# Output projection of a hybrid decoder layer: three of four units as Strassen block products, the last unit tile by tile

## The chip, the cores and the metric

The kernel runs on one core of one Trainium2 chip. The metric is the device time of one launch in microseconds (us). Engines are named as in the profile: PE (TensorE matmul), PEld (its weight loads), DVE (VectorE), ACT (ScalarE), POOL (GpSimd) and SP (SyncE). SP issues most DMAs. DMAs that add into their destination ("accumulating") are issued on POOL's queue. Sixteen DMA engines serve all queues.

## The reference

One decoder layer for 1024 tokens of width 2048. A combined projection feeds a sparse attention (heads of group A) and a chunkwise mLSTM (group B). The two results, 1024 columns each, are joined and projected, and a residual and a layer norm follow:

```python
y = jnp.concatenate([y_a, y_m], axis=-1) @ w_out[l]
x = layer_norm(ALPHA * x + y, ln_g[l], ln_b[l])
```

The change touches the product with `w_out` (2048 x 2048), how its left operand is stored, and the norm's place.

## The kernel before

All large matmuls run at about fp32 accuracy by three passes: an operand `a` is split into a rounded high part and the low rest (`split`, lines 104 to 106: a copy on ACT, a subtraction on DVE), and `mm3` (lines 108 to 111) adds high x high, high x low and low x high into one PSUM bank. One matmul here has a 128x128 stationary tile and 512 moving columns.

The stages are: the first projection groups; then 19 projection units of four column groups each and the value projection (class `Values`, lines 727 to 822), both already as Strassen block products: seven products of 512x512 blocks in place of eight, with sums of weight blocks made on DVE, POOL or by accumulating DMA (lines 631, 736); then mLSTM, then attention (lines 1097 to 1241), then the output projection (lines 1244 to 1333). `y_d` in HBM holds the transposed left operand, 16 tiles of 128 x 1024: 0 to 7 from attention, 8 to 15 from mLSTM.

The output projection runs over two halves of 512 tokens (`half`) and four blocks of 512 output columns (`cb`). One such block is 16 contraction tiles (`kt`, mLSTM's first) x 4 token tiles (`t`) x 3 passes = 192 matmuls into four banks; eight blocks make 1536. Each block loads and splits its 16 weight tiles (`load_wo`). `load_y` loads and splits the left operand, half by half. `residual` adds ALPHA x and collects statistics (`bn_stats`). `norm` finishes one token tile: six 128x512 steps on DVE, and for the column block 3 two on ACT and two on POOL, then four stores. The first half's four norms run while PE computes the second half. The last block goes token tile by token tile, so that each tile's norm runs beside the next tile's matmuls.

The order of instructions is made by a planner. It takes priorities (`tc.high_priority`) and orders (`tc.issue_after`), and it hands out the buffers of a tag as they come free: `wraw` has 6 (loaded weights), `wh` and `wl` 4 each (split weights), `s4` 11 tiles of 4 KB a partition. The pool `oq` lies where attention's pool `ap` was. Matmuls of the output projection come after attention's last logits (`last_logit`) and fill PE between attention's last blocks.

Of the kernel before, what the change touches and what calls it, by code (L numbers as in the profile page):

```python
# [19 lines left out]
P = 128  # L20
# [79 lines left out]
def kernel(ctx, tc, a, out):  # L100
# [47 lines left out]
    part_d = dp.tile([NU, P, 2, T], F32, name="part_d")  # L148
    if_d = dp.tile([2 * H_M, T], F32, name="if_d")
# [744 lines left out]

    def mlstm_store(h, j, hs, sg):
        for half in range(2):
            ps = bank("ht")
            for c in range(4):
                pe.transpose(ps[:, c * P:(c + 1) * P], hs[half][:, c, j * P:(j + 1) * P], ident)
            vec.tensor_tensor(sg[:, halves[half]], ps, sg[:, halves[half]], op=OP.mult)  # L900
        sync.dma_start(y_d[8 + 2 * h + j], sg)
# [182 lines left out]
    HT = T // 2  # L1084
    yh, yl = {}, {}

    def load_y(q, half, pool_):
        with tc.high_priority(offset=O_PRIO):
            i = half, q
            yh[i] = pool_.tile([P, 2, HT], F32R, name=f"yh{q}")  # L1090
            yl[i] = pool_.tile([P, 2, HT], F32R, name=f"yl{q}")
            for k in range(2):
                raw = wp.tile([P, HT], F32, name="wraw", tag="wraw", bufs=WR)
                sync.dma_start(raw, y_d[2 * q + k, :, half * HT:(half + 1) * HT])
                split(yh[i][:, k], yl[i][:, k], raw)

    with ExitStack() as ph:
        ap = ph.enter_context(tc.tile_pool(name="ap", bufs=2))

        def head_inputs(h):  # L1100
            tb = ap.tile([P, 640], F32, name="tb")
# [3 lines left out]
            gt = ap.tile([P, T], F32, name="gt")  # L1105
# [3 lines left out]

        diagonal = [[ap.tile([P, 512], F32R, name=f"{n}{i}", bufs=1) for n in ("dh", "dl")] for i in range(2)]  # L1110
# [3 lines left out]
        head_0 = head_inputs(0)  # L1114
        mask = []
        for t in range(8):
            w = max((t + 1) * P, 256)
            m = ap.tile([P, w], BF16, name=f"mask{t}", bufs=1)
# [6 lines left out]
            mask.append(m)  # L1125
# [15 lines left out]
        def weights(p, qk, tb):  # L1141
# [3 lines left out]
            for t in (2 * p, 2 * p + 1):  # L1145
# [6 lines left out]
                pool.tensor_tensor(nm[:, 0:ws], mask[t][:, w - ws:w], tb[:, off:off + ws], op=OP.add)  # L1152
# [36 lines left out]
        def mix(b):  # L1189
# [11 lines left out]
            if b.kk == b.p:  # L1201
                s = slice(b.p * 256, (b.p + 1) * 256)
                vec.tensor_tensor(b.gt[:, s], out_ps[0], b.gt[:, s], op=OP.mult)
                if b.end:
                    sync.dma_start(y_d[b.h], b.gt)
# [34 lines left out]
        for q in range(4, 8):  # L1240
            load_y(q, 0, op)
# [3 lines left out]
    ln = []  # L1245
    for half in range(2):
        z = []
        for t in range(4):
            r0 = half * HT + t * P
            z.append([s4("z") for _ in range(2)])  # L1250
            for i in range(2):
                (pool if half else sync).dma_start(z[t][i], a["x"][r0:r0 + P, i * T:(i + 1) * T])

        def product(ps, t, kt, wh, wl, n):
            ts = slice(t * P, (t + 1) * P)
            return mm3(ps, yh[half, kt // 2][:, kt % 2, ts], yl[half, kt // 2][:, kt % 2, ts], wh, wl,
                       n == 0, n == KT - 1)

        def residual(t, cb, ps):
            zc = z[t][cb // 2][:, (cb % 2) * 512:(cb % 2) * 512 + 512]  # L1260
            vec.scalar_tensor_tensor(out=zc, in0=zc, scalar=ALPHA, in1=ps, op0=OP.mult, op1=OP.add)
            vec.bn_stats(st[t][:, cb], zc)

        def norm(t):
            mv = oq.tile([P, 2], F32, name="mv", bufs=2)
            vec.bn_aggr(mv, st[t])
            rs = oq.tile([P, 1], F32, name="rs", bufs=2)
            tt = oq.tile([P, 1], F32, name="tt", bufs=2)
            nmean = oq.tile([P, 1], F32, name="nmean")
            act.activation(tt, mv[:, 1:2], AF.Sqrt, bias=eps)  # L1270
            refine_rsqrt(rs, mv[:, 1:2], tt)
            r0 = half * HT + t * P
            for cb in (3, 0, 1, 2):
                zc = z[t][cb // 2][:, (cb % 2) * 512:(cb % 2) * 512 + 512]
                cs = slice((cb % 2) * 512, (cb % 2) * 512 + 512)
                g, b = ln[cb // 2][:, cs], ln[2 + cb // 2][:, cs]
                if cb == 3:
                    act.mul(nmean, mv[:, 0:1], -1.0)
                    act.activation(zc, zc, AF.Identity, bias=nmean)
                    pool.tensor_tensor(zc, zc, g, op=OP.mult)  # L1280
                    act.mul(zc, zc, rs)
                    pool.tensor_tensor(zc, zc, b, op=OP.add)
                else:
                    vec.scalar_tensor_tensor(out=zc, in0=zc, scalar=mv[:, 0:1], in1=g, op0=OP.subtract, op1=OP.mult)
                    vec.scalar_tensor_tensor(out=zc, in0=zc, scalar=rs, in1=b, op0=OP.mult, op1=OP.add)
                sync.dma_start(out[r0:r0 + P, cb * 512:(cb + 1) * 512], zc)

        st = [oq.tile([P, 4, 6], F32, name="st", bufs=6) for _ in range(4)]
        order = list(range(8, 16)) + list(range(8))
# [97 lines left out]
```

## Time and profile before

| | us |
|---|---|
| median of 3 runs | 1904.15 (1898.52 to 1905.49) |
| the profiled execution's own time | 1902.39 |
| its span, first to last instruction | 1900.5 |
| PE busy | 1838.5 (97%) |
| DVE busy | 1267.8 (67%) |
| ACT busy | 919.0 (48%) |
| POOL busy | 342.0 (18%) |

The profiled execution lies between the lowest and the median run. PE is the busy engine: its duration for one matmul (some 390 ns) overlaps the next one's, so the pitch is read from the first and last start of a stretch and the number of matmuls between them. DMA share is the mean busy share of the sixteen DMA engines. The granted clock is given as a share of full speed.

### The profile page before, as it was taken

Reading aid. Unit: us, or ns where it says so; the run is one execution under the profiler, and the core shown is the slowest. Engines: PE = TensorE matmul, PEld = TensorE weight load, DVE = VectorE, ACT = ScalarE, POOL = GpSimd, SP = SyncE. Lnnn points to the kernel's source line nnn. Section 1 sums busy time; section 2 is a strip of 40 time slices with the busy share of each in tenths; the row PEclk is TensorE's granted clock in tenths of the full one; section 3 lists DMA queues with packets and bytes.
Section 4 is the critical chain, followed back from the end, with each engine's and each line's share of the span. In section 5 each row is a group of like instructions: output and inputs, shape, how many; then the busy total and the mean of one; then the engine's idle time right before and its main releaser. Section 6 shows DMA issues by size and latency. Waiting matters only on the chain.

```text
span 1900.5 us, 25648 instructions
## 1 busy us (share of the span) xinstructions
PE 1838.5 (97%) x8884; PEld 1545.1 (81%) x8884; DVE 1267.8 (67%) x2380; ACT 919.0 (48%) x1686; POOL 342.0 (18%) x330
## 2 busy tenths in 40 slices
PE   8999999999999999999999999997899999999996
PEld 7988888888877887788887887785789988888885
DVE  6254666787788778555767685756788854338627
ACT  5334445666667533522555564555666643224211
POOL 0022121010100001011323222221344500001102
PEclk9999999999999999999999999998899999999998
DMA  7255335345644657666656756465332444336712
GB/s 268 84 178 184 114 116 161 104 127 147 165 129 124 170 146 239 193 178 210 188 159 175 215 151 184 118 176 189 99 113 97 174 154 156 95 106 199 249 51 100
DMA packets 131274, 293.92 MB, mean 155 GB/s; under 512 B 14344, under 2 KB 25352, under 8 KB 125128
## 3 DMA queue, kind: packets, MB, share of 16 engines
q1 hardware_dynamic: 116744, 263.97, 42.6%
q0 software_dynamic: 14400, 28.32, 8.5%
q8 instruction: 70, 1.15, 0.2%
q14 instruction: 60, 0.49, 0.1%
HBM read 232.34 MB, written 63.04 MB: 155 GB/s over the span
## 4 chain that ended last, share of the span: by engine, by line
PE 80%; DVE 7%; DMA 7%; ACT 3%; issue 2%; SPq 0%; POOL 0%; DVEq 0%; ACTq 0%; POOLq 0%
PE pj L666 25%; PE lps L109 4%; PE lps L110 4%; PE lps L111 4%; PE pj L774 4%; PE pb L666 4%; PE pj L210 4%; PE pj L212 4%; PE pj L214 4%; PE zps L110 3%; PE zps L109 3%; PE zps L111 3%; PE sc L462 2%; PE sc L463 2%; DMA wraw<-wg 1%
## 5 line engine op out<-in xcount | busy, mean ns | idle before, releaser
L666 PE MATMUL pj<-xh,wh 128*128 128x512 f32 x912 | 358.5, 394 | 11.7 <-DVE res L675 5.7
L666 PE MATMUL pj<-xl,wh 128*128 128x512 f32 x912 | 356.0, 390 | 0.0
L666 PE MATMUL pj<-xh,wl 128*128 128x512 f32 x912 | 352.0, 391 | 1.3 <-DVE wl L657 1.2
L653 ACT CAST wh<-wraw 128x512 fp32r<-128x512 f32 x266 | 163.1, 618 | 228.7 <-PE pj L666 107.1
L657 DVE TENSOR_TENSOR wl<-wraw,wh 128x512 fp32r<-128x512 f32 x247 | 175.0, 712 | 61.9 <-ACT wh L653 43.4
L666 PEld LDWEIGHTS pj<-xh,wh 128*128 128x128 f32 x912 | 171.4, 188 | 52.1 <-DVE res L675 8.7
L666 PEld LDWEIGHTS pj<-xh,wl 128*128 128x128 f32 x912 | 171.1, 188 | 38.5 <-DVE wl L657 3.8
L666 PEld LDWEIGHTS pj<-xl,wh 128*128 128x128 f32 x912 | 171.5, 188 | 33.9
L631 POOL DMA_DIRECT2D wraw<-wg x76 | 66.4, 873 | 489.9 <-DMA wraw<-wg 241.5
L105 ACT CAST woh<-wraw 128x512 fp32r<-128x512 f32 x112 | 68.6, 620 | 157.1 <-PE lps L111 69.6
L106 DVE TENSOR_TENSOR wol<-wraw,woh 128x512 fp32r<-128x512 f32 x112 | 77.6, 705 | 97.3 <-ACT woh L105 97.3
L675 DVE TENSOR_TENSOR res<-res,pj 128x512 f32<-128x512 f32 x152 | 102.8, 680 | 50.9 <-PE pj L666 39.5
L106 DVE TENSOR_TENSOR wl<-wraw,wh 128x512 fp32r<-128x512 f32 (+4 forms) x102 | 65.3, 644 | 87.3 <-ACT wh L105 79.6
L469 DVE SCALAR_TENSOR_TENSOR sc<-r,wi,sc 128x384 f32<-128x384 f32 (+2 forms) x90 | 92.2, 1048 | 45.8 <-ACT r L464 45.3
L464 ACT ACTIVATE r<-sc 128x384 f32<-128x384 f32 (+3 forms) x160 | 79.5, 523 | 79.5 <-PE sc L463 73.7
L105 ACT CAST wh<-wraw 128x512 fp32r<-128x512 f32 (+4 forms) x102 | 55.9, 552 | 118.7 <-PE pj L212 57.6
L210 PE MATMUL pj<-xh,wh 128*128 128x512 f32 x320 | 103.7, 396 | 5.6 <-ACT xh L105 5.6
L212 PE MATMUL pj<-xl,wh 128*128 128x512 f32 x320 | 103.5, 393 | 0.0
L214 PE MATMUL pj<-xh,wl 128*128 128x512 f32 x320 | 102.8, 392 | 0.0
L590 POOL TENSOR_TENSOR wraw<-wraw 128x512 f32<-128x512 f32 x32 | 47.4, 1481 | 258.6 <-DVE st L317 110.5
L500 ACT ACTIVATE junk<-sc,cand 128x512 bf16<-128x512 f32 (+2 forms) x93 | 86.5, 931 | 6.2 <-DVE cand L515 6.0
L110 PE MATMUL lps<-wol,yh 128*128 128x512 f32 x224 | 87.7, 392 | 0.0
(343 smaller groups left out, 4397.0 us busy)
## 6 DMA issues: line engine op xcount, KB each, us to landing
wraw<-wg SPq DMA_DIRECT2D x228, 256.0 KB, 4.2
wraw<-wo SPq DMA_DIRECT2D x128, 256.0 KB, 3.0
wraw<-wg POOLq DMA_DIRECT2D x76, 256.0 KB, 5.9
part_d<-res SPq DMA_DIRECT2D x19, 1024.0 KB, 6.6
res<-part_d SPq DMA_DIRECT2D x19, 1024.0 KB, 7.7
wraw<-wv SPq DMA_DIRECT2D x48, 256.0 KB, 5.4
wraw<-xT SPq DMA_DIRECT2D x32, 256.0 KB, 2.8
wraw<-y_d SPq DMA_DIRECT2D x32, 256.0 KB, 2.8
```

Of the source, the lines that this page charges most:

```text
L105: act.copy(hi, src)
L106: vec.tensor_tensor(lo, src, hi.bitcast(F32), op=OP.subtract)
L109: pe.matmul(ps, ah, bh, start=start, stop=False)
L110: pe.matmul(ps, ah, bl, start=False, stop=False)
L111: return pe.matmul(ps, al, bh, start=False, stop=stop)
L210: pe.matmul(ps[i], wh, xh(k, i), start=k == k_first, stop=False)
L212: pe.matmul(ps[i], wh, xl(k, i), start=False, stop=False)
L214: last_mm[0] = pe.matmul(ps[i], wl, xh(k, i), start=False, stop=k == k_last)
L653: last_cast[0] = act.copy(wh, src)
L657: last_low[0] = vec.tensor_tensor(wl, src, wh.bitcast(F32), op=OP.subtract)
L666: last_mm[0] = pe.matmul(ps, w[:, k], x[:, k], start=start and k == 0 and n == 0, stop=k == 3 and n == 2, skip_group_check=True)
L675: vec.tensor_tensor(dst, dst, ps, op=OP.subtract if minus else OP.add)
```

## The change

The output projection is cut into four units by contraction half `p` (0: mLSTM's tiles of `y_d`, 1: attention's) and column half `c`. A unit multiplies 1024 x 1024 by 1024 x 1024. Units (0,0), (0,1) and (1,0) run as seven products (names b11, b21, t1, t2, b22, t3, t4) of 4 contraction tiles x 4 token tiles x 3 passes = 48 matmuls each: 336 in place of 384. Unit (1,1) stays a plain product of 384 matmuls, token tile by token tile over all 1024 tokens, with its 16 weight tiles split beforehand (`last_weights`).

Sums of blocks of `y` (`y_form`, names s1 to s4) and of weights (`weights`) are made by accumulating DMAs on POOL's queue, issued after attention's last POOL sum (`last_sum`); one weight sum (t2) is made on DVE. Signs are put into `y_d` where it is written (`y_sign`), in a DVE instruction that stood there before without a sign. Results of the units with `p` = 0 go to HBM (`z_d`); units with `p` = 1 load x, scale it on ACT, and add `z_d` by an accumulating DMA. All eight norms run beside the last unit. In attention, tables and masks are placed in another order of memory. Left out below: the removed output loop (lines 1244 to 1333, printed above), `norm` (same steps), loaders and tile bookkeeping.

```diff
+    z_d = dp.tile([2, 8, P, 2, 512], F32, name="z_d")
...
+    def y_sign(left, upper):
+
+        return -1.0 if left == upper else 1.0
...
+            vec.scalar_tensor_tensor(out=sg[:, halves[half]], in0=ps, scalar=y_sign(h < 2, half == 0),
+                                     in1=sg[:, halves[half]], op0=OP.mult, op1=OP.mult)
...
+    def y_form(p, name, pool_):
+
+        early = p == 0 and name == "s1"
+        if name in ("s2", "s4"):
+            raw = chain[0]
+        elif early:
+            raw = [s4("yraw", (P, 2, 512)) for _ in range(2)]
+            raw = [raw[k // 2][:, k % 2] for k in range(4)]
+        else:
+            raw = oq.tile([P, 4, 512], F32, name="u" if name == "s1" else "t")
+            raw = [raw[:, k] for k in range(4)]
+        if name == "s1":
+            chain[0] = raw
+        load, more = {"s1": ("a21", "a22"), "s2": (None, "a11"), "s4": (None, "a12"),
+                      "s3": ("a11", "a21")}.get(name, (name, None))
+        f = y_tiles(sp if early else pool_, name)
+        for k in range(4):
+            if load:
+                sync.dma_start(raw[k], y_rows(p, load)[k])
+            if more:
+                with tc.issue_after(last_sum[0].ins):
+                    pool.dma_start(raw[k], y_rows(p, more)[k], accum_op=OP.add)
+            split(f[0][k], f[1][k], raw[k])
+        return f
...
-                pool.tensor_tensor(nm[:, 0:ws], mask[t][:, w - ws:w], tb[:, off:off + ws], op=OP.add)
+                last_sum[0] = pool.tensor_tensor(nm[:, 0:ws], mask[t][:, w - ws:w], tb[:, off:off + ws], op=OP.add)
...
-        for q in range(4, 8):
-            load_y(q, 0, op)
+        with tc.high_priority(offset=O_PRIO):
+            for name in ("a11", "a12"):
+                Y[name] = y_by_tile(0, name, op)
...
+                for k in range(4):
+                    sync.dma_start(self.t_sum[k], a["wo"][2 * c, :, 8 * (1 - p) + k])
+
+        def weights(self, name, k):
+            c, k0 = 2 * self.c, 8 * (1 - self.p) + k
+            src = self.t_sum[k]
+            with out_prio():
+                if name == "b21":
+                    src = load_wo(c, k0 + 4)
+                elif name == "t1":
+                    self.b22[k] = load_wo(c + 1, k0 + 4)
+                elif name == "t2":
+                    vec.tensor_tensor(src, src, self.b22[k], op=OP.add)
+                elif name in ("b22", "t3"):
+                    src = self.b22[k]
+                wh = wp.tile([P, 512], F32R, name="wh", tag="wh", bufs=WB)
+                wl = wp.tile([P, 512], F32R, name="wl", tag="wl", bufs=WB)
+                (split_minus if name == "t2" else split)(wh, wl, src)
+            with out_prio(), tc.issue_after(last_sum[0].ins):
+                if name in ("b11", "b22"):
+                    pool.dma_start(src, a["wo"][c + 1, :, k0], accum_op=OP.add)
+                elif name == "t2":
+                    pool.dma_start(src, a["wo"][c, :, k0 + 4], accum_op=OP.add)
+            return wh, wl
+
...
+            def part(t, k, w):
+                ts = slice(t * P, (t + 1) * P)
+                for n, (x, y) in enumerate(((fh, w[0]), (fl, w[0]), (fh, w[1]))):
+                    pe.matmul(ps[t], x[k][:, ts], y, start=start and k == 0 and n == 0,
+                              stop=k == 3 and n == 2, skip_group_check=True)
...
+                self.z[i, n] = [s4("z", (P, 2, 512)) for _ in range(2)]
+                if self.p:
+                    for t, z in enumerate(self.z[i, n]):
+                        r0 = 4 * i + 2 * t
+                        cs = slice((2 * self.c + n) * 512, (2 * self.c + n + 1) * 512)
+                        sync.dma_start(z, a["x"][r0 * P:(r0 + 2) * P, cs].rearrange("(t p) c -> p t c", p=P))
+                        act.mul(z, z, ALPHA)
+                        pool.dma_start(z, z_d[self.c, r0:r0 + 2, :, n].rearrange("t p c -> p t c"),
+                                       accum_op=OP.add)
...
+            for t in range(4):
+                z = self.z[i, n][t // 2][:, t % 2]
+                with out_prio():
+                    if first and not self.p:
+                        if minus:
+                            act.mul(z, ps[t], -1.0)
+                        else:
+                            act.copy(z, ps[t])
+                    else:
+                        vec.tensor_tensor(z, z, ps[t], op=OP.subtract if minus else OP.add)
+                if last and self.p:
+                    vec.bn_stats(st[:, 4 * i + t, 2 * self.c + n], z)
...
+            self.product(pa, "b11", "a11", True)
+            self.add(0, 0, pa, True, True)
+            then("a11")
...
+            self.product(pb, "b21", "a12", True, True)
+            self.add(0, 0, pb, last=True)
...
+            self.product(pc, "t1", "s1", True)
+            self.add(1, 1, pc, True)
...
+            self.product(pa, "t2", "s2", False)
+            self.add(0, 1, pa, True)
...
+            self.product(pc, "b22", "s4", False)
+            self.add(0, 1, pc, last=True)
...
+            self.product(pa, "t3", "s3", False)
+            self.add(1, 1, pa, last=True)
...
+            self.product(pa, "t4", "a22", False, True)
+            self.add(1, 0, pa, True, True, last=True)
...
+    unit_0 = Product(0, 0)
+    for name in ("s1", "s2", "s4", "s3", "a22"):
+        next_form(0)(name)
+    unit_1 = unit_0.run(lambda name: None, (0, 1))
+    unit_2 = unit_1.run(next_form(1), (1, 0))
...
+        cb, k0 = {"s1": (2, 0), "s2": (3, 0), "s4": (2, 4), "s3": (3, 4)}[name]
+        with out_prio():
+            f = y_tiles(oq, name)
+            for k in range(4):
+                (split_minus if k0 else split)(f[0][k], f[1][k], load_wo(cb, k0 + k))
+                W[cb, k0 + k] = f[0][k], f[1][k]
...
+    Y["a21"] = y_by_tile(1, "a21", oq, ("u", "t"))
+    ln = {}
+    for nm in ("ln_g", "ln_b"):
         for cb in range(4):
-            last = half == 1 and cb == 3
...
+    for t in range(8):
+        i, ts = t // 4, slice(t % 4 * P, (t % 4 + 1) * P)
+        z = [unit_2.z[i, n][t % 4 // 2][:, t % 2] for n in range(2)]
+        z_1 = s4("z", (P, 2, 512))
+        sync.dma_start(z_1, a["x"][t * P:(t + 1) * P, T:].rearrange("p (n c) -> p n c", n=2))
+        act.mul(z_1, z_1, ALPHA)
+        pool.dma_start(z_1, z_d[1, t], accum_op=OP.add)
+        for n in range(2):
+            ps = bank("zps") if t % 2 else lps()
+            for kt in range(8):
+                f = Y[("a11", "a12", "a21", "a22")[2 * i + kt // 4]]
+                mm3(ps, f[0][kt % 4][:, ts], f[1][kt % 4][:, ts], *W[2 + n, kt], kt == 0, kt == 7)
+            vec.tensor_tensor(z_1[:, n], z_1[:, n], ps, op=OP.add if i else OP.subtract)
+            vec.bn_stats(st[:, t, 2 + n], z_1[:, n])
+        norm(t, z + [z_1[:, 0], z_1[:, 1]])
```

## Rows read from the trace of the kernel before

**Rows 1.** Page, part 1: busy us, share of the span, instructions of each engine.

```profile
PE 1838.5 (97%) x8884; PEld 1545.1 (81%) x8884; DVE 1267.8 (67%) x2380; ACT 919.0 (48%) x1686; POOL 342.0 (18%) x330
```

**Rows 2.** Stretches: from:to, length, busy us (instructions) by engine, clock, DMA share, GB/s.

```profile
1310.00:1340.00 30.00, 19.96 (x74) 15.03 (x75) 16.83 (x54) 14.26 (x28) 4.27 (x11) 0.66 0.60 199
...
1540.00:1580.00 40.00, 39.53 (x180) 31.93 (x178) 23.61 (x38) 20.12 (x34) 0.00 (x0) 1.00 0.67 221
...
1664.00:1708.00 44.00, 44.00 (x194) 36.26 (x194) 16.38 (x26) 10.38 (x18) 0.00 (x0) 1.00 0.32 98
...
1752.00:1796.00 44.00, 44.00 (x195) 36.28 (x194) 27.61 (x46) 11.94 (x20) 9.30 (x10) 1.00 0.85 291
...
1840.00:1885.40 45.40, 45.38 (x200) 37.08 (x198) 31.24 (x52) 6.13 (x13) 10.11 (x7) 1.00 0.21 77
1885.40:1900.50 15.10, 0.00 (x0) 0.00 (x0) 8.52 (x14) 1.83 (x4) 3.00 (x2) 0.64 0.22 83
```

**Rows 3.** Output tiles zps, lps: ns min/median/max, first and last start (us).

```profile
L109 PE MATMUL zps<-woh,yh x224: 389/391/397, 1579.1 to 1873.6; 128*128 128x512 f32 x112
...
L111 PE MATMUL lps<-woh,yl x224: 388/389/390, 1623.3 to 1885.0; 128*128 128x512 f32 x112
```

**Rows 4.** The two Strassen halves of the value projection: stretches, then PE's waits.

```profile
720.70:802.10 81.40, 77.71 (x341) 63.59 (x340) 59.15 (x75) 34.84 (x53) 6.99 (x8) 1.00 0.77 233
802.10:883.40 81.30, 81.30 (x359) 67.04 (x358) 43.72 (x68) 22.93 (x37) 8.71 (x10) 1.00 0.67 191
...
PE pj L774 <- DVE wl L764: 1.9, 1, 1.9
PE pc L774 <- DVE v L795: 1.8, 1, 1.8
```

**Rows 5.** DMA queue q0 (POOL's, here accumulating), 240 to 520 us: packets, MB, share.

```profile
q0 software_dynamic: 2736, 4.98, 11.1%
```

**Rows 6.** DMA queue q1 (SP's), 1664 to 1708 us: packets, MB, share.

```profile
q1 hardware_dynamic: 2328, 4.24, 31.2%
```

**Rows 7.** Both queues together, 822 to 826 us: packets, MB, share.

```profile
q0 software_dynamic: 287, 0.52, 70.6%
q1 hardware_dynamic: 288, 0.53, 39.9%
```

**Rows 8.** Accumulating DMA of line 631: POOL's time to issue (ns), and landing (us).

```profile
L631 POOL DMA_DIRECT2D wraw<-wg x76: 856/865/1036, 313.2 to 1279.1; - x76
...
DMA to landing us min/median/max: 4.1/5.9/9.4
```

**Rows 9.** Groups of instructions, shapes apart: busy us, mean ns, idle before.

```profile
L106 DVE TENSOR_TENSOR wol<-wraw,woh 128x512 fp32r<-128x512 f32 x112 | 77.6, 705 | 97.3 <-ACT woh L105 97.3
L105 ACT CAST woh<-wraw 128x512 fp32r<-128x512 f32 x112 | 68.6, 620 | 157.1 <-PE lps L111 69.6 <-DMA wraw<-wo 43.8 <-PE zps L111 42.3
...
L795 DVE TENSOR_TENSOR v<-v,pj 128x512 f32<-128x512 f32 x20 | 12.6, 680 | 6.4 <-PE pj L774 6.4
...
L1262 DVE BATCH_NORM_STATS2 st<-z 128x6 f32<-128x512 f32 x32 | 21.6, 686 | 0.2
```

**Rows 10.** Time line of DVE, first and last step of one token tile's norm.

```profile
1875.41 0.67 DVE L1261 SCALAR_TENSOR_TENSOR z<-z,zps 128x512 f32<-128x512 f32 x1
...
1881.14 3.11 DVE L1285 SCALAR_TENSOR_TENSOR z<-z,rs,ln_b 128x512 f32<-128x512 f32 x3
```

**Rows 11.** Time line of POOL: attention's last sum. Tile z: loads by SP.

```profile
1521.22 0.68 POOL L1152 TENSOR_TENSOR nm<-mask,tb 128x256 f32<-128x256 bf16 x1 [0.55 <-DVE mn L1159]
...
L1252 SPq DMA_DIRECT2D z<-x x8: 333/402/1097, 1482.4 to 1508.8; - x8
```

More of the change, by code (lines that the diff above doesn't have):

```diff
@@ L1083 @@
     op = ctx.enter_context(tc.tile_pool(name="op", bufs=1))
[L1084 to L1095, printed above, removed]
+    Y = {}
@@ new lines, in y_by_tile @@
+    def y_by_tile(p, name, pool_, *tags):
+        f = y_tiles(pool_, name, *tags)
+        for k, src in enumerate(y_rows(p, name)):
+            raw = wp.tile([P, 512], F32, name="wraw", tag="wraw", bufs=WR)
+            sync.dma_start(raw, src)
+            split(f[0][k], f[1][k], raw)
+        return f
+    chain, last_sum = [None], [None]
+    def y_form(p, name, pool_):
[20 more added lines that the diff above has]
+            split(f[0][k], f[1][k], raw[k])
+        return f
@@ new lines, with lps, out_prio, split_minus @@
+    st = sp.tile([P, 8, 4, 6], F32, name="st", tag="state")
+    def lps():
+        return lp.tile([P, 512], F32, name="lps")
+    def out_prio():
+        return tc.high_priority(offset=O_PRIO)
+    def split_minus(hi, lo, src):
+        act.mul(hi, src, -1.0)
+        vec.scalar_tensor_tensor(out=lo, in0=src, scalar=-1.0, in1=hi.bitcast(F32), op0=OP.mult, op1=OP.subtract)
+    def load_wo(cb, kt):
+        raw = wp.tile([P, 512], F32, name="wraw", tag="wraw", bufs=WR)
+        sync.dma_start(raw, a["wo"][cb, :, kt])
+        return raw
@@ new lines, in next_form, with then, last_weights @@
+    def next_form(p):
+        def then(name):
+            with out_prio():
+                Y[name] = y_form(p, name, op if name in ("a11", "a12") else oq)
+        return then
+    unit_0 = Product(0, 0)
[3 more added lines that the diff above has]
+    unit_2 = unit_1.run(next_form(1), (1, 0))
+    W = {}
+    def last_weights(name):
+        if name not in SUMS:
+            return
+        cb, k0 = {"s1": (2, 0), "s2": (3, 0), "s4": (2, 4), "s3": (3, 4)}[name]
+        with out_prio():
+            f = y_tiles(oq, name)
+            for k in range(4):
+                (split_minus if k0 else split)(f[0][k], f[1][k], load_wo(cb, k0 + k))
+                W[cb, k0 + k] = f[0][k], f[1][k]
@@ new lines, with norm @@
+    unit_2.run(last_weights)
+    Y["a21"] = y_by_tile(1, "a21", oq, ("u", "t"))
+    ln = {}
+    for nm in ("ln_g", "ln_b"):
+        for cb in range(4):
+            ln[nm, cb] = wp.tile([P, 512], F32, name=nm, tag="wh" if nm == "ln_g" else "wl", bufs=WB)
+            sync.dma_start(ln[nm, cb], bcast_rows(a[nm][0, cb * 512:(cb + 1) * 512]))
+    def norm(t, z):
+        mv = sp.tile([P, 2], F32, name="mv_z", tag="mv", bufs=2)
+        vec.bn_aggr(mv, st[:, t])
+        rs = sp.tile([P, 1], F32, name="rs_z", tag="rs", bufs=2)
+        tt = sp.tile([P, 1], F32, name="tt_z", tag="tt", bufs=2)
+        nmean = sp.tile([P, 1], F32, name="nm_z", tag="den", bufs=2)
+        act.activation(tt, mv[:, 1:2], AF.Sqrt, bias=eps)
+        refine_rsqrt(rs, mv[:, 1:2], tt)
+        for cb in (3, 0, 1, 2):
+            zc, g, b = z[cb], ln["ln_g", cb], ln["ln_b", cb]
+            if cb == 3:
+                act.mul(nmean, mv[:, 0:1], -1.0)
+                act.activation(zc, zc, AF.Identity, bias=nmean)
+                pool.tensor_tensor(zc, zc, g, op=OP.mult)
+                act.mul(zc, zc, rs)
+                pool.tensor_tensor(zc, zc, b, op=OP.add)
+            else:
+                vec.scalar_tensor_tensor(out=zc, in0=zc, scalar=mv[:, 0:1], in1=g, op0=OP.subtract, op1=OP.mult)
+                vec.scalar_tensor_tensor(out=zc, in0=zc, scalar=rs, in1=b, op0=OP.mult, op1=OP.add)
+            sync.dma_start(out[t * P:(t + 1) * P, cb * 512:(cb + 1) * 512], zc)
```

153 lines of the change are left out of this document (65 added, 88 removed).

## The prediction, made before the change was run

> **What bounds the kernel now.** I read the page's busy times first, then the stretches of the output projection, then one tile's first and last start, then the places where the kernel already does what the change adds. PE is busy 97% of the span [rows 1]. In the output projection it is busy 44.00 of 44.00 us and never pauses, while DVE, ACT, POOL and the DMA engines have room most of the time [rows 2]. So the stage from about 1523 to 1885 us lasts as long as its matmuls. Their pitch: from the second block's first matmul to the last one, 1579.1 to 1885.0 us [rows 3], seven blocks of 192 go by, 305.9 / 1343 = 0.2278 us each. That is the price of every matmul taken away, as long as nothing else takes over the pace. Behind the last matmul lies a tail of 15.1 us (last residual, norm, stores) [rows 2].
>
> **What is removed.** Three units fall from 384 to 336 matmuls: 144 x 0.2278 = 32.8 us, all of it on the path. Nothing else in the change shortens that path. The start stays where it is (attention's last logits), and the tail is the same chain for one last token tile.
>
> **What is added on DVE and ACT.** Splits of weights and y tiles: 128 + 32 before; after it 84 in the units (28 each), 16 for the last unit, 28 + 28 + 4 of y: again 160. At 0.705 us on DVE and 0.620 on ACT [rows 9] this cancels. New on DVE are 12 sums for t2 (0.69 each), and 68 adds of products (12 + 12 + 28 + 16) at 0.68 [rows 9] where 32 residuals stood; the 32 statistics at 0.69 [rows 9] stay. That is 8 + 46 - 22 = 32 us more for DVE, over some 340 us in which it was busy between a third and two thirds [rows 2]. The tightest stretches are the last two units. Unit 2 (76.5 us of PE): 48 splits, 4 sums, 28 adds, 16 statistics = 33.8 + 2.8 + 19.0 + 11.0 = 66.6 us. Last unit: one token tile's norm with one column block takes DVE 8.8 us [rows 10], with two blocks 10.2, against 48 matmuls = 10.9 us of PE. Both fit, at 87% and 93%. What hides them is PE's own time; if DVE enters the last unit late, the lateness is carried to the tail. The last adds of unit 2 come to 4 x 1.37 = 5.5 us, and the slack is 0.7 us a tile, so the tail grows by 0 to 5.5 us; I take 2, since most of those adds run before the product ends.
>
> **What is added on the DMA queues.** Counted in pieces of 256 KB: plain ones 48 in each Strassen unit (12 weight loads, then 20 y tiles and 16 of results in units 0 and 1, or 20 tiles for the last unit and 16 of x in unit 2) and 56 in the last (16 of x, 8 of ln, 32 of output); accumulating ones 28, 28, 28 and 16. A plain 256 KB costs the sixteen engines 31.2% x 44 / 16.2 = 0.85 us (4.24 MB are 16.2 such pieces) [rows 6], an accumulating one 11.1% x 280 / 19 = 1.64 us (4.98 MB are 19) [rows 5], nearly double for the same bytes. Sum: 200 x 0.85 + 100 x 1.64 = 334 us of all sixteen engines, 87 in each Strassen unit of 76.5 us. Taken alone that is more than a unit has. Against it: with both queues at work their shares add up to 1.10 and 1.05 MB went by in 4 us [rows 7], and the y tiles that unit 1 loads for unit 2 are due seven products later, so that an excess of 10 us a unit may run over into the last unit, which needs 74 of 87. I price this at a quarter of the excess of units 1 and 2: 5 us, with ends 0 and 21.
>
> The Trainium skill, page "DMA: Bandwidth & Descriptors", section "Anatomy of one DMA — SWDGE (gpsimd) path", gives a DMA from POOL's queue as 2.0 us plus its bytes at 436 GB/s, so 2.6 us for 256 KB, an estimate from that page. The trace has a median of 5.9 us from issue to landing for the accumulating form [rows 8], so here the row decides. By the page this part would cost nothing and the sum below would be 5 us lower.
>
> **What is added on POOL and as waits.** 100 accumulating DMAs at 0.87 us of issue [rows 8] are 87 us on a nearly idle POOL. They go in order: one that waits for a split holds back the accumulations behind it. The shortest loop is b22 to t3, which follow each other: the same tile is split, added to, and split again. With four weight buffers the first split can run 10.9 us ahead of its matmuls, and the second must end before matmuls that come another 10.9 us later: 21.8 - 2 x 1.3 for the splits leaves 19 us for 0.87 + 5.9 us, at worst 0.87 + 9.4 [rows 8]. It is covered unless the landing doubles. For the other waits of Strassen products (a product's banks, a split behind other DVE work) the value projection is the same scheme: PE was idle 81.40 - 77.71 = 3.7 us in its first half, while DVE was also finishing the key search, and 0 in the second [rows 4]. Mean 1.85 x 3 units = 5.6 us, ends 0 and 11.1.
>
> **The start.** Accumulations can't begin before attention's last POOL sum at 1521.9 us [rows 11]. s1 is needed after two products (22 us, plus attention's remaining matmuls between them) and takes some 4 x 0.87 + 5.9 + 3 = 12 us; s2 and s4 follow one product apart, with about the same chain each. Nothing should wait; I take 1 us, with ends 0 and one product, 10.9. The sign in `y_sign` changes one DVE instruction into another of the same shape: 0.
>
> **The sum.** Profiled execution 1902.4 - 32.8 + 5.6 (waits) + 5 (DMA) + 1 (start) + 2 (tail) = 1883.2. The median lies 1.8 us above that execution: **1885**. Lower end: 1904.2 - 32.8 = 1871 with no added cost, and a run may read 2 lower: 1869.
>
> **Rivals.**
> First, the DMA engines set the pace. The stage's DMAs can begin when the buffers come free, which x loads show at up to 1508.8 us [rows 11]. From there to the end of before are 391.7 us, so 334 us of DMA need a sustained share of 0.853; below that the kernel is slower than before. For: 0.85 is the highest share of any of the 44 us stretches I read [rows 2], and the value projection, which is alike, held 0.72 on the mean of its halves [rows 4]. Against: there the DMA engines weren't asked for more, and shares up to 1.10 exist [rows 7]. At a share of 0.80 the stage takes 417 us, 26 more than before: 1904 + 26 = 1930; at 0.85, 1905. PE would show waits for weights, and its clock could fall as it did to 0.66 where it was busy 20 of 30 us [rows 2], which I don't price.
> Second, waits of 1.9 us, the size of the value projection's [rows 4], stand before half of the 21 Strassen products: 10.5 x 1.9 = 20 us, and with the rest of the sum 1885 - 5.6 + 20 = 1899; before every product, 1919. For: each product changes operand, banks and weights at once, and DVE is fuller than before. Against: the second half of the value projection had none.
> Third, the change doesn't do what it says: attention's end and not PE's matmuls sets when the stage can go on, so that the time removed comes back as idle PE near 1540 to 1580 us. PE is busy 39.53 of 40 us there [rows 2], and the first two units now need nothing of attention, which speaks against it: 1904.
>
> **How the numbers follow.** 0.5% of the time, 9.5 us, is about what a measurement of this kernel can tell from no change: faster means below 1894.6, slower above 1913.7. The forecast (1869 to 1894) gets 0.66. DMA pace 0.17, of it 0.05 between 1895 and 1913 and 0.12 above. Waits 0.13: 0.03 faster, 0.07 same, 0.03 slower. The third 0.04, same. Sum: faster 0.69, same 0.16, slower 0.15. Range: 1869 to 1910, which leaves out some 0.17 above (slow DMA, a wait in every product) and a little below; the ends of the four costs together (48.5 us) would reach 1920, but they don't come all at once.
>
> **What would show it.** Right: PE's instructions fall by 144, its busy time by about 33 us, its stretches in the output projection stay full at 1.00 clock, the tail stays near 15 to 17 us, q0 carries some 26 MB more less the 4 MB of x it carried. DMA share in the middle units then stands near 0.9 or above, without waits of PE. Wrong by DMA: PE waits for `wh` or `wl` behind `wraw`, `t_sum` or y loads, landing times of accumulations far above 9 us, share well under 0.85. Wrong by waits: PE idle 1 to 3 us at product boundaries, ended by DVE or ACT. Wrong in DVE: tail over 20 us, with DVE busy throughout the last 90 us.

## The result, and the profile after

| | before | after |
|---|---|---|
| median of the runs, us | 1900.33 (1897.83 to 1905.49) | 1889.46 (1884.98 to 1891.95) |
| ratio, 95% interval | | 0.9934 (0.9914 to 0.9954) |
| profiled execution / its span, us | 1902.39 / 1900.5 | 1884.98 / 1882.9 |
| last key matmul's start to the end of the span, us | 411.1 | 398.7 |
| PE's pauses in that stretch, us | 0.5 | 16.1 |

The change is faster by 0.66%, 11 us where 19 were forecast; 1885 was forecast and 1889.5 came. The profiled execution after is the fastest of its six, 4.5 us below the median. Two spans can't be subtracted whole, though. The part ahead of the output projection, which the change hardly touches (signs, and where attention's tables and masks lie), differs from kernel to kernel. The tile `kps` (attention's keys) shows it by the start of its last matmul, the time behind "to" in these lines; first the changed kernel, then the run e8 below, whose PE instructions have the same order:

```profile
L111 PE MATMUL kps<-ch,wl x32: 389/393/628, 1314.1 to 1484.2; 128*128 128x512 f32 x32
```

```profile
L111 PE MATMUL kps<-ch,wl x32: 390/393/629, 1321.6 to 1492.5; 128*128 128x512 f32 x32
```

These starts lie between 1484.1 and 1492.5 us over all runs but e4. So the measure from here on is the time from that start to the end of the span: 1900.5 - 1489.4 = 411.1 us before, 1882.9 - 1484.2 = 398.7 after. The stage gained 12.4 us; the matmuls taken away are worth 32.8. Where did 20 us go?

The page of the changed kernel, parts 1, 3 and 4 (busy us; queues with packets, MB and share; the chain that ended last), against [rows 1]:

```profile
PE 1811.0 (96%) x8740; PEld 1522.0 (81%) x8740; DVE 1295.1 (69%) x2428; ACT 949.1 (50%) x1734; POOL 411.6 (22%) x406
...
q1 hardware_dynamic: 114632, 259.77, 42.0%
q0 software_dynamic: 26368, 50.34, 15.7%
...
PE 71%; DMA 11%; DVE 9%; issue 4%; ACT 3%; POOL 1%; SPq 1%; DVEq 0%; ACTq 0%; POOLq 0%
```

PE has 144 matmuls less, as meant (8884 - 8740), and DMA now holds 11% of the chain (7% before). The stretches, as in [rows 2]:

```profile
1540.00:1580.00 40.00, 35.56 (x156) 29.58 (x157) 25.01 (x42) 19.11 (x36) 16.24 (x20) 0.96 0.93 221
1664.00:1708.00 44.00, 40.84 (x180) 33.53 (x179) 21.60 (x35) 21.13 (x34) 10.75 (x11) 1.00 0.92 245
1708.00:1752.00 44.00, 41.10 (x172) 32.81 (x171) 25.59 (x42) 16.00 (x24) 11.88 (x13) 0.96 1.06 242
1752.00:1796.00 44.00, 41.83 (x175) 33.54 (x174) 31.39 (x52) 16.10 (x26) 2.58 (x3) 0.96 0.70 191
1840.00:1869.90 29.90, 29.88 (x132) 24.40 (x130) 27.02 (x44) 6.46 (x13) 9.84 (x7) 1.00 0.49 159
1869.90:1882.90 13.00, 0.00 (x0) 0.00 (x0) 8.60 (x15) 1.83 (x4) 2.99 (x2) 0.59 0.25 95
```

PE, the first busy time, is no longer full: 4.4 of 40 us are missing behind attention's end, 3.2, 2.9 and 2.2 in the three stretches after 1664. Three of them stand at a clock of 0.96, which is what 3.4 us at the lower level (1.2 GHz) make of 40 to 44 us: some 1.7 us more each. The tail is 13.0 us, not longer but shorter than the 15.1 of [rows 2]. PE's waits from 1490 to 1883 us (total, times, longest):

```profile
PE pb L1353 <- ACT wh L105: 4.5, 2, 3.2
PE lps L1353 <- issue: 3.3, 1, 3.3
PE pc L1353 <- ACT wh L105: 2.6, 2, 1.6
PE yps L1245 <- DVE tl L106: 2.4, 1, 2.4
PE lps L1353 <- DVE z L1390: 1.9, 1, 1.9
```

They stand in three places: at attention's end (0.8 and 2.4 us), in unit 0 (3.3 us before t2, 1.4 later), and in unit 2 (3.2, 1.3 and 1.6 us at b21 and t1). Units 0 and 1 take the first half of the contraction (mLSTM's tiles), one column half each; unit 2 opens the second half. Unit 1, from 1617 to 1693 us, has no pause. The last line is a pause of 1.9 us before t4's matmuls, ended by an addition or, in other runs, by a cast for the last unit.

PE waits for ACT's cast of a weight, but a cast takes 0.62 us. What the cast waited for shows in the chain of unit 2 (start, us, what):

```profile
1695.74 25.87 DMA z<-x
1721.61 0.02 issue
1721.63 0.04 ACT z L1376
...
1722.60 0.61 ACT wh L105
1723.21 0.04 issue
1723.25 10.55 PE pc L1353 x44
```

A load of x, issued at 1695.7, landed 25.9 us later; ACT held its scaling (line 1376) at the head of its queue for it, and the cast of the weight that PE needed stood behind. The stretch of this load:

```profile
1695.70:1721.60 25.90, 21.39 (x85) 16.57 (x84) 7.72 (x13) 9.95 (x12) 8.84 (x8) 0.93 1.10 269
```

The DMA share was 1.10. All eight loads of x of the unit were issued from 1690.3 to 1696 us, at the unit's start; the eight accumulations of `z_d` were issued from 1698.1 to 1723.6, each behind its block's scaling, and took 12.8 to 16.6 us to land.

### The profile page after: what moved, and what is told of

The parts are those of the page before. It is cut to its first block, busy times and chain, and to the rows that moved or that the text cites. A ratio compares the mean times of both kernels' runs of the same rounds, so it can differ in the third digit from the quotient of the medians.

```text
span 1882.9 us, 25521 instructions
## 1 busy us (share of the span) xinstructions
PE 1811.0 (96%) x8740; PEld 1522.0 (81%) x8740; DVE 1295.1 (69%) x2428; ACT 949.1 (50%) x1734; POOL 411.6 (22%) x406
## 3 DMA queue, kind: packets, MB, share of 16 engines
q0 software_dynamic: 26368, 50.34, 15.7%
## 4 chain that ended last, share of the span: by engine, by line
PE 71%; DMA 11%; DVE 9%; issue 4%; ACT 3%; POOL 1%; SPq 1%; DVEq 0%; ACTq 0%; POOLq 0%
PE pj L667 25%; PE pj L775 5%; PE pb L667 4%; PE lps L1353 4%; PE pj L211 4%; PE pj L215 4%; PE pj L213 4%; PE pc L775 2%; DMA wraw<-wg 2%; PE pc L1353 2%; PE sc L463 2%; PE sc L464 2%; DMA z<-x 2%; DMA wraw<-wo 1%; DMA yraw<-y_d 1%
## 5 line engine op out<-in xcount | busy, mean ns | idle before, releaser
L106 DVE TENSOR_TENSOR wl<-wraw,wh 128x512 fp32r<-128x512 f32 (+4 forms) x122 | 79.2, 655 | 127.1 <-ACT wh L105 109.1
L105 ACT CAST wh<-wraw 128x512 fp32r<-128x512 f32 (+4 forms) x122 | 67.7, 562 | 137.1 <-PE pj L213 57.6
L591 POOL TENSOR_TENSOR wraw<-wraw 128x512 f32<-128x512 f32 x32 | 47.6, 1487 | 258.5 <-DVE st L318 110.6
L651 POOL TENSOR_TENSOR wraw<-wraw 128x512 f32<-128x512 f32 x38 | 51.7, 1360 | 159.0 <-DVE wl L658 136.2
L1201 POOL TENSOR_TENSOR nm<-mask,tb 128x256 f32<-128x256 bf16 (+3 forms) x64 | 61.2, 974 | 108.1 <-DVE mn L1208 100.8
L504 DVE TENSOR_SCALAR_CACHE_REDUCE junk<-sc,cand 128x384 bf16<-128x384 f32 (+2 forms) x93 | 79.3, 875 | 0.7
```

## The experiments

Two theories. **Queues:** PE pays for transfers only where an instruction of ACT or DVE waits for a slow landing and a weight's split is queued behind it. **Pace:** the sixteen DMA engines have too much to do, and PE gets what they let through (the first rival of the prediction). All results in one table; "to the end" is the time from the last key matmul's start, "pauses" the sum of PE's pauses in it.

| run | median, us | ratio to before | to the end, us | pauses, us |
|---|---|---|---|---|
| before, second profile (b0) | 1905.07 (1 run) | | 411.7 | 0.6 |
| after | 1889.46 | 0.9934 | 398.7 | 16.1 |
| a0, after again | 1886.04 | 0.9934 (0.9917 to 0.9951) | 397.8 | 16.5 |
| e1, no scaling on ACT | 1883.82 | 0.9921 (0.9905 to 0.9936) | 397.8 | 14.2 |
| e2, s1 early | 1887.86 | 0.9929 (0.9914 to 0.9943) | 397.6 | 15.6 |
| e3, no y sums | 1882.81 | 0.9916 (0.9900 to 0.9932) | 389.1 | 9.7 |
| e4, copies (misplaced) | 1901.18 | 1.0007 (0.9995 to 1.0019) | 396.0 | 14.3 |
| e5, copies in the stage | 1894.21 | 0.9957 (0.9942 to 0.9972) | 402.7 | 17.3 |
| e6, x loads spread | 1887.88 | 0.9928 (0.9913 to 0.9943) | 398.3 | 13.9 |
| e7, x and z_d late | 1902.61 | 1.0007 (0.9997 to 1.0017) | 410.6 | 16.5 |
| e8, plain form | 1871.27 | 0.9840 (0.9820 to 0.9860) | 377.4 | 1.8 |
| e9, first unit's order | 1891.33 | 0.9950 (0.9931 to 0.9969) | 396.6 | 13.3 |
| e15, z by VectorE | 1879.92 | 0.9885 (0.9869 to 0.9902) | 388.7 | 9.6 |

In the expectations this span is counted from slightly other points (397.5 to 398.8 for the changed kernel).

### Both kernels again

> The changed kernel unaltered, as the yardstick of this group of runs and to see a second profile of it. In its first profile the output projection began 5.3 us earlier than in the kernel before (first output matmul at 1517.9 against 1523.2 us) and took 12.3 us less. Theory Q (below) and its rival D say nothing on the 5.3 us; if they belong to the order of the instructions, a second profile shows them again, if they belong to the one execution, it doesn't. Time expected 1885 to 1892.

> The kernel before, unaltered, for a second profiled execution. In the first one the first matmul of the output projection started at 1523.2 us; in two profiled executions of the changed kernel it started at 1517.9 and 1517.7. Order theory (the planner lays the instructions ahead of the output projection out differently in the two kernels): 1523 again, within 1 us. Rival (executions scatter): anything between 1517 and 1523.

The changed kernel repeated itself: the same pauses at the same matmuls, 1517.7 for the output projection's first matmul. The kernel before started it at 1525.3, outside of what either expectation allowed. e5, e6 and e8, with a0's order of matmuls up to attention's end, started it at 1523.0, 1520.8 and 1526.1. So the lead of 5 us in the first profile doesn't come from the order of PE's instructions. Whether it belongs to the changed kernel at all is open: both of its profiled executions are the fastest of their sets, 4.5 and 2.2 us below the medians. What makes the part ahead differ by up to 8 us was not followed up.

### Taking the scaling from ACT (e1)

```
-        return -1.0 if left == upper else 1.0          # y_sign
+        return -1.0 / ALPHA if left == upper else 1.0 / ALPHA
-                        act.mul(z, z, ALPHA)           # and in norm: EPS / ALPHA ** 2
```

> The scaling of x by ALPHA on ACT (16 instructions) is gone: the sum is kept divided by ALPHA through the signs in y_sign, and the norm's epsilon is divided by ALPHA squared, so the result is the same. All DMAs stay. Theory Q: PE waits because weight casts stand in ACT's queue behind ACT instructions that wait for a DMA; the scalings of unit 2 are such. Then the three gaps at 1704, 1714 and 1722 us (3.2 + 1.4 + 1.6 us) and the clock's dip after them (1.7 us) go: 7 to 8 us less than the changed kernel, about 1882. Rival D (the DMA engines, 0.9 busy, set the pace): same bytes, same time, 1889.

ACT no longer holds the weights, and the two pauses at b21 are gone, but 2.4 us at t1 and 1.8 at t2 have come. DVE's waits in unit 2, 1695 to 1765 us:

```profile
DVE z L1391 <- DMA z<-z_d: 7.3, 2, 3.9
...
DVE t_sum L1336 <- DMA wraw<-wo: 6.5, 2, 5.3
```

The next instruction that needs the landings, DVE's addition to z, now holds the low halves of the weights. The place was right, the cure was not: "to the end" stays at 397.8.

### Spreading the loads of x (e6)

```
+                        with tc.issue_after(last_wo[0].ins):
                             sync.dma_start(z, a["x"][...])     # on top of e1
-            if self.p:
-                self.block(1, 1)                               # (1, 1) after b21, as in units 0 and 1
```

> The changed kernel with 1/ALPHA taken into y_sign and ALPHA squared into the norm's epsilon, so that x needs no scaling on ACT (the result is the same), and with the x loads of the third unit issued one block at a time behind the weight loads of the product ahead, instead of all eight at the unit's start. Taking the scaling away alone gave 1883.8: the waits of that unit moved from products b21 and t1 to t1 and t2, where VectorE then held adds that waited for the accumulations into z, at a DMA share of 1.10. Queue theory (what reaches TensorE is a burst of transfers of which only a quarter is needed at once, through in-order queues): the 5.9 us of waits and the 1.7 us of half clock of that unit go, 1878 to 1880. Rival DMA pace: the bytes are the same, so the waits move once more, 1883 to 1886.

Against the queue theory, nothing was gained. The chain of unit 2:

```profile
1693.71 5.49 DMA z<-x
...
1699.80 0.91 POOL z L1381
1700.71 0.49 issue
1701.20 17.35 DMA z<-z_d
1718.55 0.02 issue
1718.58 0.04 DVE z L1394
```

x now lands in 5.5 us. The accumulation of 512 KB behind it takes 17.4 us, and DVE's addition waits for that. The burst of loads was not the cause either; the accumulation itself takes the time now. With the run that follows, that makes three in which the order was changed, the waits moved, and the sum stayed (397.6 to 398.3): where a wait ends up is a matter of the queues, that it comes is not.

### Starting s1 early (e2)

```
-                with tc.issue_after(last_sum[0].ins):
+                with ExitStack() if early else tc.issue_after(last_sum[0].ins):
```

> The changed kernel, but the four accumulations into the first row block's s1 don't wait for attention's last POOL sum; the same transfers, earlier. In the unaltered changed kernel attention's last matmuls wait 0.2 and 3.4 us for ACT and DVE, where ACT's queue holds casts of s1 that wait for those accumulations, and TensorE's clock is at half speed for 3.4 us behind that (1.7 us lost). Queue theory: these go, 4 to 5 us less, about 1881 to 1882, stage 346 to 347 us instead of 351.0. Rival DMA pace: the same bytes, so the same time, 1886, and the waits come back further on in the same unit.

The stretches from 1500 to 1540 us:

```profile
1500.00:1520.00 20.00, 17.32 (x120) 16.07 (x119) 15.47 (x41) 11.71 (x22) 11.60 (x12) 1.00 0.71 174
1520.00:1540.00 20.00, 19.65 (x134) 17.93 (x133) 13.63 (x37) 11.89 (x28) 12.39 (x14) 1.00 0.68 130
```

The wait went along with the accumulations: ACT's casts of s1 now hold attention 2.7 us at 1512.8. Nothing gained (397.6), as under the pace theory, though the DMA share there is 0.7.

### Leaving the y sums out (e3)

```
-                with tc.issue_after(last_sum[0].ins):
-                    pool.dma_start(raw[k], y_rows(p, more)[k], accum_op=OP.add)
```

The 32 accumulations into s1 to s4 are left out, so those operands hold unsummed tiles.

> The accumulating DMAs of the y sums are left out (32 pieces of 256 KB), so s1 to s4 hold wrong values; all other work stays. Theory Q: the gaps in unit 0 (0.8 + 2.4 + 3.3 + 1.0 + 0.4 us) and a clock dip (1.7 us) go, those at 1704 to 1722 us stay: 8 to 10 us less, about 1880. Rival D: 32 x 1.64 = 52 us of DMA time less, so all waits go, those of unit 2 too: 1889 - 21 = 1868.

```profile
1520.00:1540.00 20.00, 20.00 (x139) 18.42 (x138) 13.75 (x37) 10.83 (x25) 8.66 (x10) 1.00 0.44 93
1540.00:1580.00 40.00, 38.70 (x183) 31.55 (x182) 28.24 (x47) 23.88 (x43) 5.70 (x7) 1.00 0.68 200
```

The pauses at attention's end and in unit 0 fall from 8.2 to 1.8 us, those in unit 2 stay (5.8 us): 389.1, 8.7 less, as the queue theory said, and not the 21 of the pace theory. The time itself, 1882.8, is only 3.2 us below a0's, and not about 1880: the part ahead took 5.0 us longer in the profile.

### More load on the DMA engines (e4, e5)

```
+        if n < 24:                                             # e5, in load_wo
+            with tc.issue_after(loaded.ins):
+                sync.dma_start(scr[n], a["x"][n % 8 * P:(n % 8 + 1) * P, 0:T])
```

> Added: 21 plain copies of 512 KB from HBM to HBM, one at the start of each Strassen product, that nothing waits for. At the cost of plain pieces they take at least 42 x 0.85 = 36 us of all sixteen DMA engines, 12 us in each unit of 76.5 us that already asks for 87. Rival D: the time grows by most of that, 25 to 36 us, to 1915 or more. Theory Q: only the waits that exist grow with the landing times, by 3 to 8 us, to about 1895.

> The changed kernel with 24 added copies of 512 KB from DRAM to DRAM, each issued on SP behind one of the first 24 loads of wo, so that they go during attention's end and the three Strassen units; nobody reads what they write. At 0.85 us of the sixteen engines for 256 KB they ask for at least 24 x 1.7 = 41 us of all DMA engines. Rival DMA pace: the stage is longer by most of that, 20 to 41 us, 1906 to 1927. Queue theory: only the copies that fall into stretches at a share of 0.9 or more (some 40 us behind attention's end, some 40 us at the third unit's start) delay a load that a queue waits for, and the others cost nothing: 0 to 10 us, 1886 to 1896, with new waits only in those stretches.

e4 missed its place: its copies were ordered behind instructions of another engine, which held nothing back here, and all 21 went between 27 and 59 us. They say nothing of the output projection, which started some 20 us late (1538.2). In e5 each copy stands behind a load on SP, and 18 of the 24 went after 1500 us. The stretches from 1580 to 1708 us:

```profile
1580.00:1623.00 43.00, 37.72 (x156) 29.47 (x155) 20.30 (x32) 17.24 (x32) 8.77 (x11) 0.96 1.08 290
1623.00:1664.00 41.00, 41.00 (x181) 33.75 (x180) 21.38 (x33) 19.99 (x36) 9.52 (x12) 1.00 0.81 241
1664.00:1708.00 44.00, 44.00 (x196) 36.42 (x195) 24.73 (x39) 23.75 (x41) 12.39 (x15) 1.00 1.04 280
```

At a share of 1.04 and 280 GB/s PE is full for 44 us. About 31 us of DMA work (18 x 1.7, an estimate; by q1's share from 1500 to 1870 us, 45.9% against 38.5%, it was 27) cost 402.7 - 398.2 = 4.5 us, mostly where unit 0's end was already late (1.5 and 3.7 us before b22 and t3, 1.0 and 0.3 without the copies). That is within the 0 to 10 us of the queue theory and far from 20 to 41: the engines as a whole don't set the pace of the stage, and this rival falls.

### The accumulating form itself (e8)

```
-    pool.dma_start(..., accum_op=OP.add)     # all 100 pieces of 256 KB
+    pool.dma_start(...)
```

The additions are left out, transfers, bytes, queue and order stay.

> The changed kernel with all 100 accumulating pieces of the output projection as plain transfers from the same queue, at the same places and with the same bytes and waits (the additions are left out, so y sums, weight sums and the result hold other values). What falls is the price of the accumulating form, 1.64 instead of 0.85 us of the DMA engines for 256 KB: 79 us of 334. Queue theory: a wait ends as soon as the transfer in front of the queue lands, so with landings nearer to those of the plain form the 16 us of waits fall to a third or a half, 386 to 390 us from attention's last key matmul to the end (now 398), 1874 to 1878. Rival DMA pace: no wait is left, since 255 us of demand stand against 350, 380 to 384 us, 1868 to 1872. If neither, 398: the waits hang on the number of transfers and the issue on POOL, not on what each costs the DMA engines.

377.4, below what either theory forecast, and nearer to the pace theory's 380 to 384: 1.8 us of pauses, no drop of the clock in the stage before the last matmul. The DMA queue and some issues from 1500 to 1870 us (KB each, median us to landing), first the changed kernel, then e8:

```profile
q0 software_dynamic: 13120, 26.22, 39.8%
...
z<-z_d POOLq DMA_DIRECT2D x16, 512.0 KB, 11.1
...
t_sum<-wo POOLq DMA_DIRECT2D x24, 256.0 KB, 8.5
...
u<-y_d POOLq DMA_DIRECT2D x12, 256.0 KB, 10.9
```

```profile
q0 software_dynamic: 7744, 26.22, 20.7%
...
z<-z_d POOLq DMA_DIRECT2D x16, 512.0 KB, 7.3
...
t_sum<-wo POOLq DMA_DIRECT2D x24, 256.0 KB, 4.7
...
u<-y_d POOLq DMA_DIRECT2D x12, 256.0 KB, 5.8
```

The same 26.22 MB took the engines 39.8% of 370 us accumulating and 20.7% plain: 1.47 against 0.77 us for 256 KB. The plain form went in larger packets, too, but packets of one size differ as much: those of 4 KB took 364 ns accumulating (1024 of them, mean) and 190 plain. So it is the form and not the number of packets. The medians to landing fall by 28% to a half over six groups, three of them shown. So nearly all that the stage lost, 398.2 - 377.4 = 21 us, is the price of this form. How it acts, no run separates: by the landing time of each accumulation, by its POOL issue (0.86 us and more against 0.54), or by the engines' time, of which e8 saves 71 us. e5 speaks against the last alone: at its rate, 4.5 us for 27 to 31, the 71 would be worth 10 to 12 of the 21 us (an estimate).

### Moving the waits off the path (e7, e9, e15)

```
+        def fold(self, *blocks):              # e7, on top of e1: x, then z_d, accumulated into z
+            ...                               # behind the last weight accumulation; bn_stats in the last unit
```

> The changed kernel with 1/ALPHA taken into y_sign (as in the run without scaling; the result is the same), and with x and the stored partial sums z_d kept out of the third unit's queues: the first product that reaches a block is copied into z by ACT, as in the units before, x and z_d are accumulated into z behind the unit's last weight accumulation on POOL's queue, and the 16 statistics stand in the last unit. No instruction of ACT or DVE in that unit then waits for a transfer of x or z_d; the bytes are the same, and x costs the DMA engines more (1.64 instead of 0.85 us for 256 KB, 13 us in all). From attention's last key matmul to the end the changed kernel took 398.8 and 397.9 us, and 397.9 and 398.3 in the two runs in which the waits of this unit had only moved. Queue theory: the 5 to 6 us of waits and one or two drops of the clock in that unit go, 391 to 393 us, 1878 to 1881. Rival DMA pace: more DMA time, so 398 us or more, 1886 or more.

Unit 2 runs without a pause until t4, and then all comes at once. PE's only wait after 1690 us, and the chain to it:

```profile
PE lps L1355 <- DVE z L1396: 9.9, 1, 9.9
```

```profile
1758.99 13.14 DMA z<-z_d
1772.40 0.37 issue
1772.77 0.68 DVE st L1503
1773.45 0.59 DVE wl L106
1774.04 0.61 DVE z L1396
1774.78 12.38 PE lps L1355 x44
```

The planner put a statistic that needs the late accumulation ahead of the split and the addition that t4 needs, and later ones hold the norms: the tail is 27.8 us. 410.6, where the queue theory gave 391 to 393; slower than the changed kernel by 12: the same mechanism at its dearest place.

```
+    behind_weights: s4, s3, a22 of unit 0 split after the weights of t2, b22, t3     # e9
```

> The changed kernel with the first unit's splits of s4, s3 and a22 put behind the weight splits of t2, b22 and t3 on ACT and DVE; the transfers are the same. In the unaltered changed kernel ACT takes four casts of s4 and three of s3, which wait for accumulations, ahead of the last three weight casts of t2, and TensorE waits 3.2 to 3.3 us at the first matmul of t2 and 1.5 us at b22 and t3. Queue theory: these 4.7 us fall to 0 to 2.5, 395 to 396 us from attention's last key matmul to the end, 1882 to 1884. Rival (s2 itself, whose memory and sums come late, or DMA pace): the 3.2 us stay, and later splits may cost a wait at s4 or s3: 398 us or more.

The 3.3 us before t2 are gone, 2.6 us at s3's product have come: 396.6, 1.6 less than the changed kernel's mean, and the median shows nothing of it.

```
-                        pool.dma_start(z, z_d[...], accum_op=OP.add)                 # e15: e6 and e9, and
+                            sync.dma_start(part[:, 2 * t:2 * t + 2], z_d[...])       # part: y's u and t buffers
+                            vec.tensor_tensor(z[:, k], z[:, k], part[:, 2 * t + k], op=OP.add)
```

> The accumulating form taken out of the third unit's z, and the order of the first unit's splits: 1/ALPHA in y_sign, x loads one block at a time, first-unit splits behind the weight splits (each as in the runs before), and z_d loaded by plain transfers into the two buffers of 1 MB that held y sums, with 16 additions on VectorE (0.68 us each, 11 us on an engine that was busy 24 to 25 of 44 and 30 to 34 of 44 us in that unit). 32 of the 68 weight and z accumulations' bytes in the three units change form by this, and nothing is left out. Theory, that the accumulating form's slow landings reach TensorE through the in-order queues: the third unit's waits of 5 to 7 us and its one or two clock drops mostly go, the first unit's stay near 5, 388 to 392 us from attention's last key matmul to the end (the changed kernel 397.5 and 398.3), 1876 to 1881. Rival, that VectorE or any burst of transfers is what holds the queue: 396 to 398 us, 1884 to 1887, with TensorE then waiting for the added additions or for weight loads behind z_d on SP's queue.

(The pieces that change form are 16 of all 100, not 32 of 68.) PE from 1690 to 1768 us, mostly unit 2, which starts at 1701.7 here:

```profile
1690.00:1768.00 78.00, 77.11 (x339) 63.08 (x338) 54.87 (x91) 28.67 (x50) 10.49 (x12) 1.00 0.76 215
```

Unit 2's pauses fall from 6.3 to 0.9 us (the one before t4, 1.9 and 1.0 us, aside) at a full clock, DVE takes the additions at 70% of the stretch. 388.7 to the end and 1879.92 us, as forecast, ratio 0.9885 (0.9869 to 0.9902): faster than both kernels. The z accumulations, 16 of 100 pieces, were worth most of unit 2's loss. The reorderings that came along stood at 398.3 (e6) and 396.6 (e9), each by itself; together, without the change of form, they were not run. The accumulations of y at attention's end and in unit 0 (7.7 us in pauses, and 6.8 us at the lower clock) are still there.

The queue theory in its first form, that a pause goes when the waiting instruction is moved, failed in e1, e2, e6 and e7; the pace theory failed in e3 and e5. What stands is the slow landing of the accumulations, which the queues of ACT and DVE bring to PE at one place or another.

## Why the prediction was right, and where it was not

The time fell inside the range and on the side given. The gain was 10.9 of the 19.2 us forecast: the mechanism was right, some of its terms were not. That 1885 and 1889.5 lie closer together is luck in part, since before's six runs have a median of 1900.33, 3.8 us below the three that the forecast started from.

- **Matmuls, -32.8.** Right. With the plain form the stage is 411.4 - 377.4 = 34.0 us shorter than the mean of the two profiles of before, of which 1.1 lie in the tail (14.1 against 15.2).
- **Waits of products, 5.6, DMA pressure, 5, and start, 1:** 11.6 us together, against 15.6 us of pauses beyond before's 0.5. The kind was foreseen (1 to 3 us at product boundaries, ended by ACT or DVE). The step that failed is the price of the landing: it was read in a part of the kernel where an accumulation landed in 5.9 us and at worst in 9.4 [rows 8], and only the start of s1 and the loop b22 to t3 were tried against it. In the output projection the medians of the six groups are 7.4 to 11.1 us and single ones 17. That loop did hold (0.2 to 0.7 us at t3 in two profiles), and the waits arose where the prediction didn't look: at the in-order queues of ACT and DVE, where casts of y sums and additions to z wait for accumulations, and scalings of x for loads that run beside them, ahead of weights' splits. The 5 us of DMA pressure had another reason, more work than the engines do in a unit, and e5 bears that out only in small part.
- **The figure of the Trainium skill.** The Trainium skill, page "DMA: Bandwidth & Descriptors", section "Anatomy of one DMA — SWDGE (gpsimd) path", gave an estimate of 2.6 us for 256 KB. Plain pieces from POOL's queue took 4.7 us here (the median of `t_sum` in e8; the shortest took 2.9), accumulating ones 8.5: the rows decide, against the page.
- **Clock, not priced:** three stretches at 0.96, about 5 us. The prediction named a falling clock for its first rival alone, but it fell behind pauses of 1.9, 2.4 and 3.2 us.
- **Tail, +2:** it fell by 2.1 (13.0 against 15.1). The additions of unit 2 didn't run over: DVE was busy 58% and 71% in the stretches from 1708 and 1752 where 87% had been counted, since the splits of a11 and a12 lay ahead of the unit and the waits made it longer, and the last unit kept PE full. The fall itself is none of DVE's: from the last matmul to DVE's last step it is 8.8 us before and 8.9 after, and behind that, with the last stores, 6.3 and 4.1. Why these were shorter was not followed up.
- **Sum:** -32.8 + 15.6 + 5 - 2.1 = -14.3, against -12.4 measured from the last key matmul. Most of the gap of 2 us lies in how pauses are counted: from the end of a matmul, 0.39 us behind its start, while the next would have started after 0.23 us, so each of the ten costs some 0.16 us more (an estimate, 1.6 us in all).
- **First rival (DMA engines):** refuted as a pace (e5), though its first condition, the double price of an accumulation, is what the change paid: 1.47 us a piece here, 1.64 had been read from [rows 5]. All in all the two queues took 78% of 370 us, 290 us, where 334 had been counted.
- **Second rival (waits before half of the products):** pauses of over 1 us stood before or in 5 of the 21 products (t2 and b22 of unit 0, b21, t1 and t4 of unit 2), so the likeliest case was nearer.
- **Third rival (attention's end):** its place was right and its reason was not: 3.2 us came back there, by s1's casts in ACT's queue.

What the prediction named as signs of being right held where they concerned counts (144 matmuls, q0 at 50.34 MB) and the DMA share (0.90 and 0.93 in unit 0's stretches, 0.92 over unit 2, though 0.80 over unit 1); it failed at stretches that "stay full at 1.00 clock" and at the tail. Of its signs for "wrong by DMA", PE's waits for `wh` and landings far above 9 us came, and the share under 0.85 did not.

## What to carry to other kernels

An addition by accumulating DMA is free only in bytes: price it by its landing at the place where it will run, with everything issued beside it, and follow the first instruction that waits for it to what is queued behind on that engine. When a pause moves instead of ending as the order is changed, it is the slow producer that must go; where an engine has time to spare, let it add. Compare stages from a common point, since the part ahead can scatter by more than the effect.

## What the hardware showed that was not expected

- The same bytes took 13120 packets accumulating and 7744 plain, at 1.9 times the DMA engines' time, and packets of 4 KB alone show the same factor (364 against 190 ns); a POOL issue of 256 KB took 0.86 us and up to 3.3 accumulating, 0.54 plain.
- Accumulations of 512 KB landed in 12.8 to 16.6 us in the changed kernel's unit 2 (17.4 in e6), and in 5.4 to 9.4 in its last unit. There they went in packets of 4 KB instead of 2, POOL's issue took 0.86 us instead of 1.20, and the DMA share was 0.60 instead of 0.92; which of these counts was not tried.
- Of the eight pauses of 1.9 to 3.4 us in the two profiles of the changed kernel, five were followed by 3.4 us at the lower clock level (1.2 GHz), and three were not, among them the longest of unit 0, 3.2 and 3.3 us before t2.
